# The first modulation by halves of the features, and the v product ahead of gates, q and k

## The chip, the core and the metric

The kernel runs on one core of one Trainium2 chip. The metric is the device time of one execution in microseconds. The program holds 352 MB of DMA traffic and 28,462 instructions. TensorE (PE) does matrix products, VectorE (DVE) and ScalarE (ACT) do elementwise work, GpSimd (POOL) does a little, and SyncE (SP) issues the DMAs that bring weights from memory.

## The reference

The reference is two transformer-like blocks on a sequence of 256 tokens with 1024 features, batch 1. Only the start of the first layer matters here:

```
c_act = silu(c)
mod = c_act @ ada_w[i] + ada_b[i]
sh1, sc1, g1, sh2, sc2, g2 = split(mod, 6)
h = rmsnorm(x, norm_g[i, 0]) * (1.0 + sc1) + sh1
# mlstm_mixer (layer 0):
p = h @ w_in
q, k, v, o, ig, fg = split(p)          # 512, 512, 1024, 1024, 8, 8 columns
... gates from ig, fg: cumulative decay, a running maximum, a masked decay matrix
scores = (q k^T) * decay;  num = scores @ v;  hh = num / denominator, normed
out = (sigmoid(o) * hh) @ w_out
x = x + g1 * rmsnorm(out, norm_g[i, 1])
h = rmsnorm(x, norm_g[i, 2]) * (1.0 + sc2) + sh2      # then the feed-forward part
```

`sh1` and `sc1` are one vector of 1024 numbers each, and every product of the mixer needs them. They come from `c_act` times 1024 x 1024 weights each, 4 MB for each of the two.

## The kernel before

Activations are kept transposed in SBUF: features on the 128 partitions, eight feature chunks (`KD`) of 128, and 256 tokens along the free dimension. A product in float32 accuracy is done as three fp32r products: the activation and the weight are each split into a rounded part `hi` (a ScalarE cast) and a rest `lo` (a VectorE subtraction, the method `split`), and hi*hi, hi*lo and lo*hi are summed in PSUM. `weights` loads one 1 MB tile of weights (`st`, 128 x 2048 float32) from the pool `wst`, a ring of three buffers, and makes the two pairs hi/lo of 128 x 1024. A buffer of the ring is free again when its last reader on VectorE is done.

Order in `first_block`, layer 0:

1. `ada_start` is called four times, b = 0 to 3: shift features 0 to 511, shift 512 to 1023, scale 0 to 511, scale 512 to 1023. Each call brings 2 MB of `ada_w` as four DMAs of 512 KB in two buffers `st`. Of its eight feature chunks four go through float32 matmuls against a broadcast of `c_act` (`crep`), four are summed on VectorE into `s`, and a last float32 matmul with a matrix of ones adds `s`. `diagonal` picks the column out of the PSUM tile (a product with the identity and a reduction on VectorE), and the bias is added.
2. `Finish.whole` does the RMS norm of X (`chain`: squares on ScalarE, a power on GpSimd, the scaling on VectorE and ScalarE), turns the normed rows (`turn`: float32 transposes on PE, then `hf` = scale * xn + shift) and then runs `Head`: the gate columns (40 of them) and the first two of the eight q/k blocks as float32 matmuls straight from `hf` and unsplit weights. The splits of `hf` come after.
3. `mlstm`: gates on ScalarE and VectorE, with three activation table loads; the running maximum `M` goes to memory (`md`) and comes back broadcast to all partitions (`mx`, 1.5 MB); six remaining q/k blocks by `dense_b` (24 matmuls of 256 columns each); the v product by `dense_a` (96 matmuls of 512 columns); then the o product (`a_w_o`, another 96) interleaved with the eight attention heads; then `a_w_out`.

Beside these, `self.side` holds generators for later modulations (g1, sh2, sc2). `pump` runs a step of the first of them when it is called: a step loads 1 MB of `ada_w` and multiplies it into `s` with two VectorE instructions (or a ScalarE one and a VectorE one). `mlstm` calls `pump` twice among the q/k blocks, four times in the v product and three times in the o product; the `a_w_out` product calls it with three steps at a time, and before its last weights `drain` runs whatever is left. The instructions are put in an order per engine when the program is built; each engine then runs its own in that order, and SP issues the DMAs in that order and waits where a buffer is not free.

Of the kernel before, what the change touches and what calls it, by code (L numbers as in the profile page):

```python
# [10 lines left out]
F32 = mybir.dt.float32  # L11
# [5 lines left out]
AF = mybir.ActivationFunctionType  # L17
ALU = mybir.AluOpType
# [4 lines left out]
D = 1024  # L23
KD = 8
# [251 lines left out]
class Net:  # L276
# [62 lines left out]
    def setup(self):  # L339
        nc, c, a = self.nc, self.const, self.a  # L340
        self.cols = c.tile([128, NCOL], F32, name="cols")
        nc.sync.dma_start(self.cols, a["cols"])
        self.X = self.keep.tile([128, 2, D], F32, name="X")
        k = c.tile([128, 6, 128], F32, name="kc")
        nc.sync.dma_start(k, a["k128"])
        self.junk = self.const.tile([128, D], BF16, name="junk")
        self.ident, self.ones, self.mbig, self.anti, self.bdiag, self.iota = (k[:, i] for i in range(6))
        self.cand_iota = c.tile([128, NCAND], F32, name="ciota")
        nc.sync.dma_start(self.cand_iota, a["ciota"])
# [23 lines left out]

    def weights(self, ap):

        n = ap.shape[1]
        st = self.load(ap)
# [115 lines left out]

    def ada_start(self, i, b, o):

# [5 lines left out]
        for h in range(2):  # L501
            st = self.wst.tile([128, 2048], F32, tag="st", name="st").rearrange("p (k n) -> p k n", k=4)
            for q in range(2):
                nc.sync.dma_start(st[:, 2 * q:2 * q + 2], w[2 * h + q])
            for k in range(4):
                kk = 4 * h + k
# [117 lines left out]

    def mlstm(self, x, pump, finish):
        nc, a = self.nc, self.a
        with ExitStack() as es:
# [37 lines left out]
            for n2 in range(4):  # L665
                for j, ps in enumerate(self.pair(x, a["a_w_qk"], n2, 1)):
                    n = 2 * n2 + j
# [5 lines left out]
                if n2 == 2:  # L673
# [10 lines left out]
            for t in range(2):  # L684
                for h in range(2):
                    nc.scalar.copy(v[:, t, 4 * h:4 * h + 4, :128], acc[t][h].rearrange("p (h d) -> p h d", h=4))
            hh = mp.tile([128, 2, 8, 129], F32, name="hh")
# [175 lines left out]


    def first_block(self):
        with self.tc.tile_pool(name="adap", bufs=2) as self.ada_p, self.tc.tile_pool(name="wsx", bufs=2) as self.wsx:
            m0, first, rest = self.ada_mods(0)
            with self.tc.tile_pool(name="crep", bufs=1) as p:
                self.crep = p.tile([128, KD, 128], F32, name="crep")
                self.nc.vector.tensor_copy(self.crep, self.cact.unsqueeze(2).to_broadcast([128, KD, 128]))  # L870
                for b in range(4):
                    self.ada_start(0, b, m0["sh1" if b < 2 else "sc1"][:, 4 * (b % 2):4 * (b % 2) + 4])
                    if b == 0:
                        self.nc.sync.dma_start(self.X, self.a["x"].rearrange("o (t p) d -> p (o t) d", p=128))
                o = m0["sc1"]
                self.nc.vector.scalar_tensor_tensor(o, o, 1.0, self.col("ng0_0"), op0=ALU.add, op1=ALU.mult)
            with self.tc.tile_pool(name="st0", bufs=2) as p, self.tc.tile_pool(name="work", bufs=1) as work:
# [3 lines left out]
            x = self.mlstm(fin.x, 2.0, lambda p, hst: Finish(self, p, m0["g1"], m0["sc2"], m0["sh2"], head=self.pairs(self.a["ffn_w1"][0], 4), head_pool=hst))  # L881
            m1, first, rest1 = self.ada_mods(1)
# [697 lines left out]
```

## Time and profile before

| | us |
|---|---|
| three runs, median (lowest to highest) | 1742.36 (1741.71 to 1742.83) |
| the profiled execution's own time | 1743.49 |
| its span, first to last instruction | 1741.2 |
| PE busy in the span | 1708.2 (98%) |
| DVE busy | 1378.5 (79%) |
| ACT busy | 917.5 (53%) |

The page cuts the span into 40 slices of 43.5 us. PE is busy 9 tenths or more in all but the first (7) and the last (8).

### The profile page before, as it was taken

How to read it: one execution, taken by the hardware profiler on the slowest of the kernel's cores; microseconds unless marked ns; L12 is line 12 of the kernel's file. 1: busy time of each engine (PE TensorE's matmuls, PEld its weight loads, DVE VectorE, ACT ScalarE, POOL GpSimd, SP SyncE). 2: the span in 40 equal slices, each digit the busy share in tenths (PEclk: the TensorE clock that was granted, in tenths of full speed). 3: DMA queues.
4: the chain of work that ended last, by engine and by line, in shares of the span. 5: the costliest groups of instructions: out<-in, count | busy, mean ns of one | idle time of the engine just before them, and what ended most of it. 6: DMA issues, size and time to landing. Idle time of an engine off the chain costs nothing.

```text
span 1741.2 us, 28462 instructions
## 1 busy us (share of the span) xinstructions
PE 1708.2 (98%) x11306; PEld 1508.9 (87%) x11306; DVE 1378.5 (79%) x2399; ACT 917.5 (53%) x1519; POOL 29.8 (2%) x43
## 2 busy tenths in 40 slices
PE   7999999999999999999999999999999999999998
PEld 3877888888888888999899999999888997878886
DVE  5687988679758555999867999799788948888754
ACT  3565665664456565566544445444443444445543
POOL 0000000000000000000000000000000000000000
PEclk9999999999999999999999999999999999999999
DMA  9886888558628653544355555545554455554751
GB/s 332 302 296 247 334 312 324 215 194 301 231 82 330 211 193 106 177 146 170 117 186 168 185 189 175 173 167 171 180 182 163 154 187 176 187 175 167 254 193 45
DMA packets 59599, 352.42 MB, mean 202 GB/s; under 512 B 6165, under 2 KB 12613, under 8 KB 19273
## 3 DMA queue, kind: packets, MB, share of 16 engines
q1 hardware_dynamic: 59466, 350.61, 56.7%
q8 instruction: 88, 1.44, 0.3%
q14 instruction: 45, 0.37, 0.1%
HBM read 349.51 MB, written 1.07 MB: 201 GB/s over the span
## 4 chain that ended last, share of the span: by engine, by line
PE 86%; DVE 7%; DMA 2%; ACT 2%; issue 2%; POOL 1%; SPq 0%; DVEq 0%; ACTq 0%; POOLq 0%
PE acc L113 38%; PE mm L397 10%; PE mm L399 10%; PE mm L398 10%; PE mm L426 6%; PE head L135 3%; PE mm L428 3%; DVE lo L366 2%; DVE yc L936 1%; DMA st<-in_ada_w_dram 1%; PE sd L1233 1%; PE sd L1244 1%; PE sd L512 1%; DVE ada L538 1%; DMA st<-in_a_w_v_dram 1%
## 5 line engine op out<-in xcount | busy, mean ns | idle before, releaser
L365 ACT CAST hi<-st 128x1024 fp32r<-128x1024 f32 (+1 forms) x507 | 523.8, 1049 | 434.1 <-PE mm L398 202.4
L366 DVE TENSOR_TENSOR lo<-st,hi 128x1024 fp32r<-128x1024 f32 (+1 forms) x507 | 612.6, 1222 | 146.8 <-ACT hi L365 145.2
L397 PE MATMUL mm<-h,hi 128*128 128x256 f32 x1544 | 443.1, 287 | 0.7 <-ACT qz L670 0.7
L399 PE MATMUL mm<-h,lo 128*128 128x256 f32 x1544 | 437.0, 283 | 0.9 <-DVE lo L366 0.9
L398 PE MATMUL mm<-h,hi 128*128 128x256 f32 x1544 | 436.9, 283 | 0.0
L397 PEld LDWEIGHTS mm<-h,hi 128*128 128x128 f32 x1544 | 295.4, 191 | 1.8 <-ACT qz L670 0.9
L399 PEld LDWEIGHTS mm<-h,lo 128*128 128x128 f32 x1544 | 295.3, 191 | 1.1 <-DVE lo L366 1.1
L398 PEld LDWEIGHTS mm<-h,hi 128*128 128x128 f32 x1544 | 295.5, 191 | 0.2
L113 PE MATMUL acc<-hi,h 128*128 128x512 f32 x768 | 229.7, 395 | 2.7 <-ACT h L365 1.8
L113 PE MATMUL acc<-lo,h 128*128 128x512 f32 x544 | 170.8, 391 | 0.1
L113 PEld LDWEIGHTS acc<-hi,h 128*128 128x128 f32 x768 | 141.9, 188 | 32.4 <-ACT h L365 3.2
L426 PE MATMUL mm<-h,hi 128*128 128x512 f32 x456 | 162.5, 400 | 0.0
L113 PE MATMUL acc<-hi,vh 128*128 128x512 f32 x448 | 142.5, 399 | 0.1
L113 PE MATMUL acc<-lo,vh 128*128 128x512 f32 x448 | 138.8, 391 | 0.0
L113 PE MATMUL acc<-hi,vl 128*128 128x512 f32 x448 | 137.9, 389 | 0.0
L113 PEld LDWEIGHTS acc<-lo,h 128*128 128x128 f32 x544 | 101.8, 188 | 21.8 <-DVE lo L366 0.5
L428 PE MATMUL mm<-h,lo 128*128 128x256 f32 x399 | 112.0, 281 | 0.5 <-DVE lo L366 0.5
L113 PEld LDWEIGHTS acc<-hi,vl 128*128 128x128 f32 x448 | 84.1, 188 | 18.4
L113 PEld LDWEIGHTS acc<-lo,vh 128*128 128x128 f32 x448 | 84.1, 188 | 18.1
L113 PE MATMUL acc<-hi,l 128*128 128x512 f32 x320 | 99.0, 390 | 0.0
L426 PEld LDWEIGHTS mm<-h,hi 128*128 128x128 f32 x456 | 84.1, 188 | 17.0 <-issue 0.7
L538 DVE SCALAR_TENSOR_TENSOR ada<-st,cact,ada 128x1024 f32<-128x1024 f32 x74 | 94.5, 1277 | 3.4 <-ACT ada L536 1.4
(397 smaller groups left out, 2187.7 us busy)
## 6 DMA issues: line engine op xcount, KB each, us to landing
st<-in_peer_u_dram SPq DMA_DIRECT2D x64, 1024.0 KB, 4.9
st<-in_peer_v_dram SPq DMA_DIRECT2D x64, 1024.0 KB, 4.9
st<-in_ffn_w_dram SPq DMA_DIRECT2D x62, 1024.0 KB, 6.2
st<-in_ada_w_dram SPq DMA_DIRECT2D x40, 1024.0 KB, 5.0
st<-in_ada_w_dram SPq DMA_DIRECT2D x16, 512.0 KB, 6.3
st<-in_b_w_u_dram SPq DMA_DIRECT2D x8, 1024.0 KB, 6.4
st<-in_b_w_v_dram SPq DMA_DIRECT2D x8, 1024.0 KB, 4.8
st<-in_b_w_out_dram SPq DMA_DIRECT2D x8, 1024.0 KB, 5.0
```

Of the source, the lines that this page charges most:

```text
L113: ins = mm(self.t[t][j], a[:, ts], b[:, j * 512:(j + 1) * 512], start=first and a is xh and b is wh, stop=last and a is xl)
L135: net.nc.tensor.matmul(ps[:, t * 128:(t + 1) * 128], w[:, k], x(k), start=k == 0, stop=k == KD - 1)
L365: i = self.nc.scalar.copy(hi, src)
L366: return i.ins, self.nc.vector.tensor_tensor(lo, src, hi.bitcast(F32), op=ALU.subtract).ins
L397: mm(out, ahi, bhi, start=start, stop=False)
L398: mm(out, ahi, blo, start=False, stop=False)
L399: return mm(out, alo, bhi, start=False, stop=stop)
L426: i = mm(ps, wh[:, k], x2[:, k], start=first, stop=last)
L428: i = mm(ps[:, :T], wl[:, k], xh[:, k], start=False, stop=False)
L512: nc.tensor.matmul(ps, self.crep[:, kk], st[:, k], start=kk == 0, stop=False)
L538: nc.vector.scalar_tensor_tensor(s, w, c, s, op0=ALU.mult, op1=ALU.add)
L936: nc.vector.scalar_tensor_tensor(y[:, n], up[:, n, w:w + T], self.col("conv_w", n * 31 + w), y[:, n], op0=ALU.mult, op1=ALU.add)
```

## The change

`ada_start` is called in the order 0, 2, 1, 3, so that shift and scale of features 0 to 511 come first. A new function `lead` replaces `Finish.whole`. It loads X ahead of most of the weights, norms both token tiles into buffers of their own, transposes and modulates features 0 to 511 (`turn(0)`, `scaled(0)`), and runs the v product over the first half of the features (`product(0)`, `product(1)`: 48 matmuls) around the third `ada_start`; after the fourth it modulates features 512 to 1023 and runs the other half of v. The weights of v go through a pool of two buffers of their own (`st0`). `mlstm` gets the finished accumulators of v, computes the gates as a split fp32r product and all eight q/k blocks by `dense_b`. `Head` is not used there any more. The constants are cut in parts that are loaded at three times. `mlstm` calls `pump` once after each q/k pair and three times in the o product.

```diff
-        nc.sync.dma_start(self.cols, a["cols"])
...
+        c8 = c.tile([128, KD], F32, name="c8")
+        nc.sync.dma_start(c8, a["cols"][:, :KD])
...
-        nc.scalar.activation(self.cact, self.col("c"), AF.Silu)
+        nc.scalar.activation(self.cact, c8, AF.Silu)
+    def fetch(self):
+        nc.sync.dma_start(self.k2, a["k128"][:, :2])
+        nc.sync.dma_start(self.X, a["x"].rearrange("o (t p) d -> p (o t) d", p=128))
+        nc.sync.dma_start(self.cols, a["cols"])
...
-    def mlstm(self, x, pump, finish):
+    def mlstm(self, x, acc, pump, finish):
...
+            for t in range(2):
+                for h in range(2):
+                    nc.scalar.copy(v[:, t, 4 * h:4 * h + 4, :128], acc[t][h].rearrange("p (h d) -> p h d", h=4))
...
-            ps = self.head.ps[0]
+            w = self.weights(a["a_w_g"])[0]
+            ps = self.dense_b(x, [t.rearrange("p (k m) -> p k m", k=KD) for t in w], m=40)
...
-                for j, ps in enumerate(self.pair(x, a["a_w_qk"], n2, 1)):
+                for j, ps in enumerate(self.pair(x, a["a_w_qk"], n2)):
...
-                if n2 >= 2:
-                    self.pump(pump)
-
-            acc = self.dense_a(x, a["a_w_v"], pump=pump)
...
+                self.pump(pump)
...
+            self.ada_start(0, 0, sh[:, :4], self.fetch)
+            self.ada_start(0, 2, sc[:, :4])
+            for t in range(2):
+                chain(t)
+            pss = turn(0)
+            scaled(0, pss)
+            pss = turn(1)
+            product(0, st0)
+            self.ada_start(0, 1, sh[:, 4:])
+            product(1, st0)
+            self.ada_start(0, 3, sc[:, 4:])
+            scaled(1, pss)
+            product(2, st0)
+            product(3, st0)
+            self.fetch_more()
...
-                for b in range(4):
-                    self.ada_start(0, b, m0["sh1" if b < 2 else "sc1"][:, 4 * (b % 2):4 * (b % 2) + 4])
...
-                fin = Finish(self, work, None, m0["sc1"], m0["sh1"], head=[(self.a["a_w_g"], 1, 40)] + self.pairs(self.a["a_w_qk"], 2), head_pool=p)
-                fin.whole()
+                v = self.lead(m0)
```

On PE, before, the last modulation matmuls (`sd<-st,crep`, and with the ones `sd<-ada,kc`) and the transposes stand ahead of the float32 head, and the first q/k block follows:

```order
L203 MATMUL mm<-kc,xn 128x128 x4
L512 MATMUL sd<-st,crep 128x512 x2
L513 MATMUL sd<-ada,kc 128x512
L203 MATMUL sd<-kc,xn 128x128 x4
L135 MATMUL head<-hf,st 40x128 x8
L135 MATMUL head<-hf,st 128x128 x16
```

On PE, now, where the v product (`acc<-hi,h_121`) begins: it stands between matmuls of the third modulation part.

```order
L528 MATMUL sd<-ada,kc 128x512
L527 MATMUL sd<-st,crep 128x512
L909 MATMUL mm<-kc,xn_122 128x128 x4
L909 MATMUL mm<-kc,xn_123 128x128 x4
L527 MATMUL sd<-st,crep 128x512
L113 MATMUL acc<-hi,h_121 128x512 x4
```

Further on, now, at the end of the first half of v and the start of the second (the matmuls with the ones, L528, stand directly ahead of the second half):

```order
L113 MATMUL acc<-hi,h_121 128x512 x2
L527 MATMUL sd<-st,crep 128x512 x4
L528 MATMUL sd<-ada,kc 128x512
L113 MATMUL acc<-hi,h_121 128x512 x2
L113 MATMUL acc<-lo,h_121 128x512 x2
```

The head is gone from this place, and the four matmuls of the fourth modulation part come after all 48 of the first half of v.

On VectorE, before, in the last product of the mixer (`a_w_out`): `ada_1000` is the sum for sc2, `lo_1194` and `lo_1218` belong to the second and third MB of `a_w_out`.

```order
L749 TENSOR_TENSOR og_1095<-og_1095,hh_748 128x512 x2
L538 SCALAR_TENSOR_TENSOR ada_1000<-st_1187,cact_96,ada_1000 128x1024
L366 TENSOR_TENSOR h2_1104<-sd_1112,h2_1104 128x4x128
L366 TENSOR_TENSOR lo_1194<-st_1191,hi_1193 128x1024
L366 TENSOR_TENSOR h2_1104<-sd_1126,h2_1104 128x4x128
L366 TENSOR_TENSOR lo_1198<-st_1191,hi_1197 128x1024
L550 TENSOR_REDUCE sc2_0_107<-sd_1201 128x4
L366 TENSOR_TENSOR lo_1218<-st_1215,hi_1217 128x1024
```

On VectorE, now, at the same place (`ada_1216` is the sum for sc2, `lo_1228` the second MB of `a_w_out`, `lo_1246` the third):

```order
L379 TENSOR_TENSOR lo_1228<-st_1221,hi_1227 128x1024
L379 TENSOR_TENSOR h2_1124<-sd_1146,h2_1124 128x4x128
L553 SCALAR_TENSOR_TENSOR ada_1216<-st_1231,cact_96,ada_1216 128x1024
L565 TENSOR_REDUCE sh2_0_106<-sd_1203 128x4
L567 TENSOR_TENSOR sh2_0_106<-sh2_0_106,cols_86 128x8
L553 SCALAR_TENSOR_TENSOR ada_1216<-st_1235,cact_96,ada_1216 128x1024 x2
L553 SCALAR_TENSOR_TENSOR ada_1216<-st_1239,cact_96,ada_1216 128x1024 x2
L379 TENSOR_TENSOR lo_1246<-st_1243,hi_1245 128x1024
L565 TENSOR_REDUCE sc2_0_107<-sd_1253 128x4
```

Two more loads of the side work, and the end of sh2, have moved into this product, and six multiply-adds stand between the second and the third MB of its weights.

## Rows read from the trace of the kernel before

**Rows 1.** The page: span, busy time, chain of work that ended last

```profile
span 1741.2 us, 28462 instructions
PE 1708.2 (98%) x11306; PEld 1508.9 (87%) x11306; DVE 1378.5 (79%) x2399; ACT 917.5 (53%) x1519; POOL 29.8 (2%) x43
PE 86%; DVE 7%; DMA 2%; ACT 2%; issue 2%; POOL 1%; SPq 0%; DVEq 0%; ACTq 0%; POOLq 0%
```

**Rows 2.** Busy time by stage: stretch, length, engines, granted clock, DMA share, GB/s

```profile
core 0: us, PE busy (x) PEld busy (x) DVE busy (x) ACT busy (x) POOL busy (x), PEclk, DMA share, GB/s
36.30:49.40 13.10, 13.03 (x97) 11.68 (x97) 10.28 (x17) 8.34 (x16) 0.00 (x0) 0.87 0.95 342
49.40:93.50 44.10, 42.66 (x253) 36.76 (x252) 31.42 (x32) 25.16 (x39) 2.10 (x3) 1.00 0.84 306
93.50:128.40 34.90, 33.41 (x183) 28.36 (x181) 31.27 (x65) 23.98 (x66) 4.08 (x3) 1.00 0.81 292
128.40:156.80 28.40, 24.90 (x117) 19.49 (x116) 22.69 (x37) 11.87 (x20) 1.67 (x3) 1.00 0.78 309
```

**Rows 3.** The same view, short stretches around the start of the head

```profile
10.00:15.00 5.00, 4.93 (x8) 1.72 (x6) 1.43 (x3) 0.59 (x2) 0.00 (x0) 1.00 1.03 403
34.00:35.00 1.00, 0.21 (x3) 0.20 (x3) 0.91 (x2) 0.00 (x0) 0.00 (x0) 1.00 1.28 250
38.00:39.00 1.00, 1.00 (x6) 0.89 (x5) 0.54 (x2) 1.00 (x4) 0.00 (x0) 0.50 0.99 410
41.00:42.00 1.00, 1.00 (x11) 1.00 (x11) 1.00 (x3) 1.00 (x2) 0.00 (x0) 1.00 1.05 262
```

**Rows 4.** Timeline of the start: start, length, engine, line, operation, [idle before]

```profile
7.34 6.74 PE L512 MATMUL sd<-st,crep 128*128 128x512 f32 x8 [7.34 <-DMA st<-in_ada_w_dram]
...
8.59 0.75 DVE L510 SCALAR_TENSOR_TENSOR ada<-st,cact,ada 128x512 f32<-128x512 f32 x1 [0.87 <-DMA st<-in_ada_w_dram]
...
14.41 0.63 ACT L164 ACTIVATE junk<-X 128x512 bf16<-128x512 f32 x1 [11.04 <-DMA X<-in_x_dram]
...
17.54 0.72 ACT L192 ACTIVATE xn<-X,rs_r 128x512 f32<-128x512 f32 x1 [1.18 <-POOL rs_r L170]
...
32.99 1.02 PE L513 MATMUL sd<-ada,kc 128*128 128x512 f32 x2
...
34.05 0.69 DVE L521 TENSOR_TENSOR adad<-sd,kc 128x512 f32<-128x512 f32 x1 [1.22 <-PE sd L513]
...
35.90 2.90 ACT L216 ACTIVATE hf<-mm,sh,sc 128x128 f32<-128x128 f32 x8 [5.19 <-DVE sc L876]
...
38.65 2.21 ACT L365 CAST h<-hf 128x512 fp32r<-128x512 f32 x4
...
40.72 3.92 ACT L365 CAST hi<-st 128x1024 fp32r<-128x1024 f32 x4
```

**Rows 5.** Timeline of PE: the head here, q/k blocks, a later head, 512-column matmuls

```profile
36.37 13.26 PE L135 MATMUL head<-hf,st 128*40 128x128 f32 x96 [0.91 <-DVE hf L212]
...
49.70 0.28 PE L399 MATMUL mm<-h,lo 128*128 128x256 f32 x1
...
49.82 0.28 PE L397 MATMUL mm<-h,hi 128*128 128x256 f32 x1
...
147.30 1.75 PE L113 MATMUL acc<-hi,h 128*128 128x512 f32 x7
...
159.71 7.31 PE L135 MATMUL head<-hf,st 128*128 128x128 f32 x64
```

**Rows 6.** Timeline: the gates' maximum goes to memory, and its broadcast is used

```profile
57.13 0.30 SPq L653 DMA_DIRECT2D md<-M  x1
...
68.16 1.22 DVE L659 TENSOR_TENSOR mx<-mx,kc 128x1024 f32<-128x1024 f32 x1 [0.23 <-DMA mx<-md]
```

**Rows 7.** Timeline of the last product of the mixer: PE's largest wait, a side step

```profile
135.59 1.06 PE L484 MATMUL sd<-kc,og 128*128 128x128 f32 x8 [1.37 <-DVE og L749]
...
135.97 1.28 DVE L538 SCALAR_TENSOR_TENSOR ada<-st,cact,ada 128x1024 f32<-128x1024 f32 x1
```

More of the change, by code (lines that the diff above doesn't have):

```diff
@@ L372, in load, with weights @@
         return st
-    def weights(self, ap):
+    def weights(self, ap, stage=None):
         n = ap.shape[1]
-        st = self.load(ap)
+        st = self.load(ap, stage)
         out = []
@@ L504, in ada_start @@
                 nc.sync.dma_start(st[:, 2 * q:2 * q + 2], w[2 * h + q])
+            if h == 0:
+                then()
             for k in range(4):
@@ L862, in sgu, with lead, chain, turn @@
         return fin.x
+    def lead(self, m0):
+        nc, a = self.nc, self.a
+        sh, sc, ng = m0["sh1"], m0["sc1"], self.col("ng0_0")
+        with self.tc.tile_pool(name="st0", bufs=2) as st0, self.tc.tile_pool(name="work", bufs=1) as p:
+            x = self.h_tiles()
+            xn = [p.tile([128, D], F32, name=f"xn{t}") for t in range(2)]
+            acc = Acc(self, KD, tail=2)
+            def chain(t):
+                X = self.X[:, t]
+                ss = self.small.tile([128, 2], F32, tag="ss", name="ss")
+                for h in range(2):
+                    hs = slice(h * 512, (h + 1) * 512)
+                    nc.scalar.activation(self.junk[:, hs], X[:, hs], AF.Square, scale=1.0 / 32.0, accum_out=ss[:, h:h + 1])
+                v = self.small.tile([128, 1], F32, tag="rs_v", name="rs_v")
+                nc.vector.tensor_scalar(v, ss[:, 0:1], ss[:, 1:2], EPS, op0=ALU.add, op1=ALU.add)
+                r = self.small.tile([128, 1], F32, tag="rs_r", name="rs_r")
+                nc.gpsimd.tensor_tensor(r, v, self.mhalf, op=ALU.pow)
+                nc.vector.tensor_scalar(xn[t][:, :512], X[:, :512], r, None, op0=ALU.mult)
+                nc.scalar.activation(xn[t][:, 512:], X[:, 512:], AF.Copy, scale=r)
+            def turn(h):
+                pss = []
+                for t in range(2):
+                    ps = self.mm_tile().rearrange("p (k c) -> p k c", k=4)
+                    for k in range(4):
+                        kk = 4 * h + k
+                        nc.tensor.transpose(ps[:, k], xn[t][:, kk * 128:(kk + 1) * 128], self.ident)
+                    pss.append(ps)
+                return pss
+            def scaled(h, pss):
+                hs = slice(4 * h, 4 * h + 4)
+                nc.vector.scalar_tensor_tensor(sc[:, hs], sc[:, hs], 1.0, ng[:, hs], op0=ALU.add, op1=ALU.mult)
+                for t, ps in enumerate(pss):
+                    hf = p.tile([128, 4, 128], F32, tag="hf", name="hf", bufs=2)
+                    for k in range(4):
+                        gk, sk = sc[:, 4 * h + k:4 * h + k + 1], sh[:, 4 * h + k:4 * h + k + 1]
+                        if t == 0:
+                            nc.vector.tensor_scalar(hf[:, k], ps[:, k], gk, sk, op0=ALU.mult, op1=ALU.add)
+                        else:
+                            nc.scalar.activation(hf[:, k], ps[:, k], AF.Identity, scale=gk, bias=sk)
+                    o = (slice(None), hs, slice(t * 128, (t + 1) * 128))
+                    self.hi, self.lo = self.split(x[0][o], x[1][o], hf)
+            def product(k2, pool=None):
+                for j, w in enumerate(self.weights(a["a_w_v"][k2], pool)):
+                    k = 2 * k2 + j
+                    acc.add((x[0][:, k], x[1][:, k]), w)
+            self.ada_start(0, 0, sh[:, :4], self.fetch)
+            self.ada_start(0, 2, sc[:, :4])
+            for t in range(2):
+                chain(t)
[10 more added lines that the diff above has]
+            self.fetch_more()
+        return x, acc.t
@@ L870, in first_block @@
                 self.nc.vector.tensor_copy(self.crep, self.cact.unsqueeze(2).to_broadcast([128, KD, 128]))
[L871 to L879 removed]
+                v = self.lead(m0)
             self.side = rest[:3]
[L881 removed]
+            x = self.mlstm(*v, 2.0, lambda p, hst: Finish(self, p, m0["g1"], m0["sc2"], m0["sh2"], head=self.pairs(self.a["ffn_w1"][0], 4), head_pool=hst))
             m1, first, rest1 = self.ada_mods(1)
```

19 lines of the change are left out of this document (11 added, 8 removed).

## Prediction

> **What bounds the kernel now.** I read the page first: PE is busy for 98% of the span and holds 86% of the chain that ended last [rows 1]. So the time is PE's work plus the little that PE waits, and a change counts by what it does to those two until the last place where order differs, the end of the mixer at about 157 us. After that both kernels run the same program, PE-bound, and a lead or a lag at 157 us is carried to the end.
>
> Next the view of busy time by stage [rows 2]. The reader is to see four stages behind the modulation: the float32 head (36.3 to 49.4, at a mean granted clock of 0.87), q/k blocks and v (44.1 us, PE idle 1.4), the o product with the heads (34.9, idle 1.5) and the last product `a_w_out` (28.4, idle 3.5). Before 36.4 us PE only does float32 modulation matmuls and transposes, and DMA moves 403 GB/s [rows 3]. The largest wait of PE is there, not behind it.
>
> Then the timeline of the start [rows 4]: the first 512 KB of `ada_w` let PE go at 7.3 us, X is there at 14.4, and the last matmul with the ones begins at 33.0; 2.9 us later ScalarE writes `hf`. The head runs from 36.4 [rows 5].
>
> **The change, part by part.** All times count from the span's start, and I build the new sequence by adding durations of these rows.
>
> *Weights at the start.* Ahead of the first `ada_w` now lie 4 KB of constants instead of 0.59 MB (331 + 768 + 54 float32 on 128 partitions, from the diff). At 0.403 MB per us [rows 3] that is 1.5 us, and two issues fewer at 0.3 each [rows 6] give 0.6: the first 512 KB land at about 5 us. X ends 1.7 MB later, at 9.3. All that the first half of the features needs is 5.55 MB, so it lands at 5 + 5.03/0.403 = 17.5 us.
>
> *First half of the modulation.* DVE does not reach that DMA time, because the norm of X stands in its order among the modulation sums. X to the first `xn` takes 3.9 us (14.4 to 18.3 [rows 4]); the second tile, by the same kinds of instruction, about 2.4 more: 15.6 us. Then one sum (0.75), the ones (1.02), product and reduction (2 x 0.69), three sums (0.75 each) lead to 21.2, where the second matmul with the ones begins. From there to `hf` it takes 2.9 us as before [rows 4]: 24.1. ScalarE writes four `hf` (half of 2.90), makes two casts of h (0.55 each) and one of weights (0.98): PE can begin v at 27.6 us. I allow 26.5 to 29.
>
> *First half of v on PE.* 48 matmuls of 512 columns at 0.227 us each (seven end 1.75 after their start, the last with a tail of 0.39 [rows 5]) are 10.9 us. Between them stand eight float32 matmuls of the other two modulation parts, at about 0.87 each (bounded by the 1.02 with tail [rows 4]): 7.0. PE is through at 45.5 us. No transfer is late for it: by bytes the fourth part is there at about 35 us.
>
> *The new wait.* The second `hf` needs the ones that begin at 44.6, so it starts at 47.5; `hf`, casts of h and of weights follow (1.45 + 1.1 + 0.98): 51.0. PE has nothing else in its order there (gates and q/k stand behind v and need all of h), so it idles 5.5 us. Queued behind this wait are all of v's second half, gates and q/k.
>
> *TensorE's clock.* Before, PE was busy 0.21 of the stretch 34 to 35, and the granted clock then fell to 0.50 (1.2 GHz) at 38 to 39 and was 1.00 (2.4 GHz) again at 41 to 42 [rows 3]; the head's mean of 0.87 over 13.1 us [rows 2] costs 1.7 us at most. The 5.5 us gap is longer, so I charge 1.4 us for one fall after it, and 0.7 (half a chance of another) for the thin stretch before 27.6. The Trainium skill ("TensorE: Matmul & The Clock Gate", section "HAM oscillation — how this bites in real kernels") says that PE waits between bursts bring the throttled clock back, so that each burst starts cold; that speaks against a change that cuts the lead into two bursts. By that rule both falls come and the sum would be 0.7 us higher; the row shows one fall after one thin stretch.
>
> *Gates, q and k.* The head goes: 96 instructions in 13.1 us, of which 10.9 is work at full clock (64 in 7.31 [rows 5]). In its place come three blocks of 24 fp32r matmuls at 0.12 (from 49.70 to 49.82 [rows 5]), 8.6 us: 2.3 us less work. Second half of v 10.9 with the clock's 2.1: v ends at 64.0; nine blocks (25.9) and four tiny transposes: 90.1 us. Before, this point was 93.5. But the two float32 matmuls of g1 (1.8) now come behind it, since side steps moved: the work done is ahead by 1.6 us only.
>
> *Side work.* `pump` is called seven times ahead of `a_w_out` instead of nine. So two steps, 2 MB of `ada_w` and four multiply-adds (one on ScalarE), and the end of sh2 (eight transposes, 0.9 us at the head's rate, and two reductions) go from the earlier stages into `a_w_out`. The o stage: 34.9 + 1.8 - 0.9, less 0.8 of its 1.5 idle (some of it stood behind sh2's reductions) = 35.0: end at 125.1 against 128.4. In the last stage PE's largest wait is for `og` (1.37 [rows 7]), which DVE has ready 7.6 us into the stage; one multiply-add fewer stands ahead of it: 6.3. Behind it DVE has about 4.3 of splits, six multiply-adds of 1.28 [rows 7] and two reductions (1.3): it hands sc2's sum to PE 19.5 us into the stage. PE is there after 17.0 (6.2 for the first transposes and their wait, 35 matmuls 7.9, 20 transposes and their waits 2.9), waits 2.5, and has 0.9 + 48 x 0.227 = 11.8 left: 31.3 instead of 28.4. Bounds of this 2.9 us: +0.9, if only the transposes count, and +10.4, if both loads come in series (2.6 of transfer and 2.6 of DVE each). I take 2.9, near the rows' order. It takes back nearly all.
>
> *Constants, v copies, mask.* The copies of v move from before the o product to behind v: ScalarE was idle for much of that stage (25.2 of 44.1 busy [rows 2]), so 0; if not, up to 4 x 0.5 from the cast row's half. Later constants: not needed before `mx`, 0.
>
> **Sum.** 125.1 + 31.3 = 156.4 against 156.8 where the stage ended: -0.4, I say -0.5 us. Against the profiled execution's 1743.5 that is 1743.0; the runs' median is 1.1 lower, so I predict 1741.9. Unknown are the start of v (1.2 either way), the clock (-2.1 to +2), the last stage (-2 to +7.5).
>
> **Rivals.**
>
> *The gain stays (faster).* No clock is lost after the gap, and the side steps hide in the last stage but for their 0.9. Then 2.1 and 2.0 come on top: -4.6, 1737.8. For it: DMA moves only 309 GB/s of 403 in the last stage [rows 2, 3] and DVE idles 5.7 us there; against: DVE's multiply-adds now stand ahead of the third MB's split.
>
> *The ring of three buffers (slower).* `a_w_out`'s third and fourth MB get their buffers only when DVE has used the side loads ahead of them. If each such load costs transfer plus DVE in turn, the last stage takes 7.5 us more than I gave it: up to +7, at half of that +3.3; I price the case at +5, 1747.4. It decides from the point where sc2's sum is ready 23.5 us into the stage or later. For it: the order; against: two loads are in flight at a time.
>
> *The gates' chain comes late (slower).* Before, `M` left at 57.1 and its mask was added at 68.2 [rows 6], 25 us ahead of its use. Now it leaves about 9.6 us after v's end (7.7 as from the head's end before, and two copies of v), and by the same 12.2 us to the masked `mx`, six exponentials (2.5) and a cast the first o weights are ready 25.3 us after v's end; PE wants them at 27.5. With 2.2 us of cover it costs nothing; from 6.2 late it makes the kernel slower, and 7 late gives +4.3, 1746.7.
>
> *It does not do what it says:* if the first half of v waited for the second half's weights, v would run from 51 on: 10.9 us later on PE, 1752. Nothing in the order asks for that, so it gets almost no weight.
>
> **How the numbers follow.** What counts as no change is 0.2%, 3.5 us on 1742.4. Forecast, 1738.9 to 1745.9: 0.49. The gain stays: 0.28. The ring: 0.14. The gates' chain: 0.08; the last rival: 0.01. So faster 0.28, same 0.49, slower 0.23. The range reaches into both sides: from 1736.5 (below the first rival's 1737.8 by the start of v) to 1747.4, the ring's price.
>
> **What would show it.** In the changed kernel's timeline: v's first matmul at 26.5 to 29; a PE gap of 4 to 7 us near 45 to 51 that ends with the ScalarE cast, and a granted clock of 0.50 behind it; the o product from 88 to 92; the end of `a_w_out`'s matmuls within 3 us of 156.8; PE waiting for DVE at sc2's transposes. If the gap is absent, or the last stage takes less than 30 us, I am wrong towards faster; if it takes over 35, or PE waits for the first o weights, towards slower.

## The result: 12 us slower, and the profile after

The changed kernel takes 1754.83 us (median of 4 runs, 1754.31 to 1756.86) against 1742.58 for the kernel before: ratio 1.0069, 95% interval 1.0056 to 1.0081. The forecast was no change, 1741.9; the time lies above the range.

The page of the profile after (span; PE's busy time; the chain that ended last), to be held against [rows 1]:

```profile
span 1752.6 us, 28431 instructions
PE 1713.2 (98%) x11282; PEld 1513.3 (86%) x11282; DVE 1381.6 (79%) x2403; ACT 920.1 (52%) x1522; POOL 32.6 (2%) x43
PE 87%; DVE 7%; ACT 2%; issue 1%; DMA 1%; POOL 1%; SPq 0%; DVEq 0%; ACTq 0%; POOLq 0%
```

The span grew by 11.4 us. PE's idle time is the span less its busy time: 33.0 before, 39.4 now, +6.4. PE's busy time grew by 5.0, although PE has 24 instructions fewer. An instruction that takes longer points to the clock.

Busy time by stage in the kernel after (columns as in [rows 2]):

```profile
36.30:49.40 13.10, 12.29 (x42) 7.48 (x40) 4.62 (x9) 0.00 (x0) 0.00 (x0) 1.00 0.64 214
49.40:94.20 44.80, 39.94 (x269) 36.51 (x269) 33.63 (x39) 29.60 (x48) 2.10 (x3) 0.92 0.78 286
94.20:129.80 35.60, 34.75 (x182) 28.67 (x180) 30.48 (x62) 24.60 (x66) 6.01 (x3) 1.00 0.74 269
129.80:164.20 34.40, 28.30 (x129) 22.40 (x128) 28.41 (x44) 11.24 (x19) 1.94 (x2) 0.95 0.86 336
```

Against [rows 2] the o stage begins 0.7 us later, takes 0.7 longer, and the last product 6.0 longer (34.4 for 28.4). The granted clock is 0.92 and 0.95 where it was 1.00. Short stretches of the same view show where it was low:

```profile
28.00:31.00 3.00, 3.00 (x8) 1.71 (x7) 3.00 (x5) 3.00 (x4) 0.00 (x0) 0.52 1.00 388
53.00:58.00 5.00, 3.74 (x8) 2.54 (x9) 4.83 (x6) 5.00 (x7) 0.00 (x0) 0.50 0.31 129
151.00:154.00 3.00, 3.00 (x12) 2.61 (x11) 2.21 (x2) 2.52 (x3) 0.00 (x0) 0.50 1.02 426
168.00:171.00 3.00, 3.00 (x16) 3.00 (x16) 2.15 (x5) 2.47 (x8) 0.00 (x0) 0.51 0.43 178
```

There are four falls to 1.2 GHz where [rows 3] show one. Busy time by (1 - clock) is what a fall took from PE: 1.4 + 1.9 + 1.5 + 1.5 = 6.3 us in these four stretches, and 7.2 with their edges (windows of 2 us: 1.7, 2.3, 1.5 and 1.7); the fall before took 1.6 by the same windows. Each stands behind a wait of PE. Timeline of PE in the kernel after (idle before the row and its releaser in brackets; 67.61 is the first matmul of the gates, 94.20 the first of the scores):

```profile
13.05 2.08 PE L527 MATMUL sd<-st,crep 128*128 128x512 f32 x2 [3.26 <-DMA st<-in_ada_w_dram]
...
27.16 1.12 PE L909 MATMUL mm<-kc,xn 128*128 128x128 f32 x8 [2.31 <-ACT hf L923]
...
29.28 1.14 PE L113 MATMUL acc<-hi,h 128*128 128x512 f32 x1
...
47.57 1.02 PE L528 MATMUL sd<-ada,kc 128*128 128x512 f32 x2
54.22 1.22 PE L113 MATMUL acc<-hi,h 128*128 128x512 f32 x2 [5.63 <-ACT hi L378]
...
67.61 0.28 PE L410 MATMUL mm<-h,hi 128*40 128x256 f32 x1
...
94.20 0.60 PE L711 MATMUL sd<-qz,kT 128*128 128x256 f32 x2
...
150.64 1.63 PE L564 MATMUL sd<-kc,ada 128*128 128x128 f32 x8 [2.73 <-DVE ada L553]
...
166.44 0.33 PE L203 MATMUL mm<-kc,xn 128*128 128x128 f32 x1 [2.21 <-ACT xn L192]
```

Behind the last product PE is 7.4 us late (164.2 for 156.8); X's transposes wait 2.21 (1.12 before), the head behind them starts at half clock, and `ffn` begins 9.7 us late. The last 1.7 us of the lag come from a fall between 856 and 862 us, behind code that is the same in both kernels:

```profile
856.00:862.00 6.00, 5.83 (x36) 5.62 (x36) 3.77 (x8) 2.51 (x4) 0.70 (x1) 0.72 0.01 3
```

With it the falls took 8.9 us of PE's busy time in the whole execution, against 1.6 before. That is 7.3 more, and less 2.3 us of work (the forecast's figure for the head's loss) it gives the 5.0 by which PE's busy time grew. The 6.4 of idle time make up the rest of the 11.4. The late fall need not belong to the change: profiles of `no_head_filled` and `before_consts_late`, which keep the old order, have one like it at 840 to 846 us.

### The profile page after: what moved, and what is told of

Read it like the earlier page. It is cut to its first block, busy times and chain, and to the rows that moved or that the text cites. A ratio compares the mean times of both kernels' runs of the same rounds, so it can differ in the third digit from the quotient of the medians.

```text
span 1752.6 us, 28431 instructions
## 1 busy us (share of the span) xinstructions
PE 1713.2 (98%) x11282; PEld 1513.3 (86%) x11282; DVE 1381.6 (79%) x2403; ACT 920.1 (52%) x1522; POOL 32.6 (2%) x43
## 3 DMA queue, kind: packets, MB, share of 16 engines
HBM read 349.52 MB, written 1.07 MB: 200 GB/s over the span
## 4 chain that ended last, share of the span: by engine, by line
PE 87%; DVE 7%; ACT 2%; issue 1%; DMA 1%; POOL 1%; SPq 0%; DVEq 0%; ACTq 0%; POOLq 0%
PE acc L113 39%; PE mm L410 10%; PE mm L411 10%; PE mm L412 10%; PE mm L439 6%; PE head L135 3%; PE mm L441 3%; DVE lo L379 2%; DVE yc L1012 1%; PE sd L1309 1%; PE sd L1320 1%; PE sd L527 1%; DMA st<-in_ada_w_dram 1%; DVE ada L553 1%; PE sd L855 0%
## 5 line engine op out<-in xcount | busy, mean ns | idle before, releaser
L410 PE MATMUL mm<-h,hi 128*128 128x256 f32 (+1 forms) x1568 | 449.8, 287 | 0.0
L412 PE MATMUL mm<-h,lo 128*128 128x256 f32 (+1 forms) x1568 | 443.7, 283 | 0.9 <-DVE lo L379 0.9
L411 PE MATMUL mm<-h,hi 128*128 128x256 f32 (+1 forms) x1568 | 443.6, 283 | 0.0
L410 PEld LDWEIGHTS mm<-h,hi 128*128 128x128 f32 (+1 forms) x1568 | 299.4, 191 | 1.2 <-issue 0.6
L412 PEld LDWEIGHTS mm<-h,lo 128*128 128x128 f32 (+1 forms) x1568 | 299.3, 191 | 1.1 <-DVE lo L379 1.1
L411 PEld LDWEIGHTS mm<-h,hi 128*128 128x128 f32 (+1 forms) x1568 | 299.5, 191 | 0.3
L441 PE MATMUL mm<-h,lo 128*128 128x256 f32 x399 | 112.1, 281 | 0.5 <-DVE lo L379 0.5
L439 PEld LDWEIGHTS mm<-h,hi 128*128 128x128 f32 x456 | 84.1, 188 | 17.0 <-issue 0.7
```

The costliest lines, as they stand in the source:

```text
L410: mm(out, ahi, bhi, start=start, stop=False)
L411: mm(out, ahi, blo, start=False, stop=False)
L412: return mm(out, alo, bhi, start=False, stop=stop)
L439: i = mm(ps, wh[:, k], x2[:, k], start=first, stop=last)
L441: i = mm(ps[:, :T], wl[:, k], xh[:, k], start=False, stop=False)
```

## The experiments

Each kernel ran beside the kernel before; the ratio is to that. "Lost" is the sum of (1 - granted clock) times 2 us over windows of 2 us from 20 to 190 us of the profiled execution; it counts idle time too. Ahead of 20 us five profiles have another fall that is not in the column (`before_seven_steps` 1.0; `parts_first` and `one_burst_filled` 1.7; `before_consts_late` and `two_steps_no_dve` 3.4). "Scores" is where the first scores start in the same execution; in the old order that is inside the v product, in the kernel before 5.0 us ahead of the o product. "Last" is the length of the last product. These three columns are of one execution, which is not always near the median: that of `nine_steps` took 1751.02 us, that of `one_burst` 1751.11.

| kernel | median us | ratio, interval | lost | scores | last |
|---|---|---|---|---|---|
| before | 1742.6 to 1743.9 | 1 | 1.7 | 88.6 | 28.3 |
| after | 1754.83 | 1.0069 [1.0056, 1.0081] | 8.5 | 94.2 | 34.4 |
| nine_steps | 1754.11 | 1.0065 [1.0050, 1.0079] | 5.1 | 97.3 | 29.6 |
| before_seven_steps | 1748.73 | 1.0031 [1.0019, 1.0043] | 5.8 | 89.2 | 33.0 |
| parts_first | 1754.07 | 1.0062 [1.0047, 1.0078] | 8.6 | 87.6 | 37.1 |
| parts_first_nine | 1749.32 | 1.0036 [1.0024, 1.0048] | 3.4 | 96.7 | 29.7 |
| gap_filled | 1752.35 | 1.0059 [1.0046, 1.0072] | 3.4 | 91.4 | 34.6 |
| one_burst | 1754.41 | 1.0071 [1.0058, 1.0084] | 6.8 | 91.1 | 34.5 |
| two_steps_no_dve | 1750.29 | 1.0045 [1.0031, 1.0059] | 5.1 | 95.2 | 30.7 |
| two_steps_small_loads | 1754.38 | 1.0069 [1.0056, 1.0082] | 8.5 | 94.4 | 37.1 |
| waits_filled | 1750.40 | 1.0037 [1.0023, 1.0051] | 3.4 | 90.1 | 36.3 |
| nine_small_loads | 1749.60 | 1.0032 [1.0018, 1.0045] | 5.1 | 95.9 | 29.6 |
| before_consts_late | 1744.26 | 0.9999 [0.9987, 1.0011] | 0 | 89.5 | 28.3 |
| before_no_head | 1749.43 | 1.0030 [1.0019, 1.0041] | 5.1 | 91.8 | 29.1 |
| no_head_seven_steps | 1748.65 | 1.0030 [1.0018, 1.0041] | 6.8 | 92.1 | 32.7 |
| before_ten_steps | 1744.99 | 1.0010 [1.0001, 1.0019] | 3.4 | 84.4 | 28.7 |
| parts_nine_spare | 1748.51 | 1.0037 [1.0025, 1.0049] | 3.4 | 95.9 | 28.8 |
| no_head_filled | 1744.12 | 1.0005 [0.9997, 1.0014] | 0 | 88.8 | 28.3 |
| one_burst_filled | 1752.16 | 1.0052 [1.0039, 1.0065] | 5.1 | 90.0 | 35.9 |
| before_spare | 1745.66 | 1.0014 [1.0005, 1.0023] | 0 | 88.4 | 28.3 |

**The displaced side steps.** `nine_steps` adds to the changed kernel's q/k loop:

```diff
+                if n2 >= 2:
+                    self.pump(pump)
                 self.pump(pump)
```

> The changed kernel with nine instead of seven side steps ahead of the last product (one step more behind each of the third and fourth pair of q and k). Theory A, the displaced side steps: the two steps that the change moved into the last product cost it its 6 us and, by the waits there, the clock falls behind it. Then the last product goes from 34.5 back to 28.5 to 31 us, the wait of PE for sc2's sum and the falls at 151 and 168 us go, and the whole is 6 to 10 us shorter than the changed kernel (1745 to 1749). Theory B, the lead in two bursts costs it (the gap of 5.6 us at 48.6 and the clock after it, which only hid behind an earlier start): the whole stays within 2 us of the changed kernel (1753 to 1757), since nothing ahead of 68 us is touched.

The last product came back to 29.6 us and its falls went, as theory A said, but the scores start 3.1 later and the median is unchanged, as theory B said. In the profiled execution the mixer still ends 1.0 earlier (163.2 for 164.2) and `ffn` begins 3.1 earlier; the other four executions were 2 to 5 us longer than that one. So the trace shows that most of the gain is paid back among q and k, and not where the rest of it goes. `before_seven_steps` takes `if n2 >= 2: self.pump(pump)` out of the kernel before.

> The kernel before, with two side steps fewer ahead of the last product (the two behind the third and fourth pair of q and k are left to it), so that its 18 steps divide as in the changed kernel; nothing else is changed. Theory A: slower than the kernel before by 5 to 10 us (1748 to 1753), with PE waiting in the last product for sc2's sum. Theory B: within 2 us of the kernel before (1741 to 1745).

+5.7 us, in theory A's range, but not by the wait that it named: PE has no wait for sc2's sum there. Its longest in the last product is for `og`:

```profile
130.01 0.63 PE L484 MATMUL sd<-kc,og 128*128 128x128 f32 x4 [2.18 <-DVE og L747]
```

Its last product is 4.7 longer and its stretch from the scores to there 3.9 shorter (125.2 less 89.2, for 128.5 less 88.6), so the mixer ends only 1.4 later (158.2 for 156.8). "Lost" is 5.8 for 1.7. That points to the clock behind the waits for much of the price; no run fills these waits.

To see what a displaced step uses, the last two of sc2 lost first VectorE's products, then most of their loads (with products of the same size over the 64 columns that are left; these lines are not shown):

```diff
-            for k in range(2):
+            for k in range(0 if (i, b) == (0, 4) and h >= 2 else 2):
```

```diff
-            st = self.load(self.a["ada_w"][i, b, h], self.ast)
+            few = (i, b) == (0, 4) and h >= 2
+            st = self.load(self.a["ada_w"][i, b, h][:, :64] if few else self.a["ada_w"][i, b, h], self.ast)
```

> The changed kernel without VectorE's four products of the last two steps of sc2 (1.3 us each); their loads of 1 MB each remain. Left out: half of the sum behind sc2. It prices the displaced steps by their engine. If VectorE's time in the o stage and the last product is what they cost (theory A): the last product goes from 34.5 to 28 to 30 us and the whole is 5 to 9 us shorter (1746 to 1750). If it is their loads (theory C): the last product stays at 32 us or more and the whole within 3 us of the changed kernel.

> The counterpart: the changed kernel with the loads of the last two steps of sc2 cut from 1 MB each to 32 KB each, and VectorE's four products of the same size over what is loaded, repeated. Left out: the weights of these two steps. Theory C (loads): the last product at 28 to 30 us and the whole 5 to 9 us shorter than the changed kernel. Theory A (VectorE's time): 33 us or more, the whole within 3 us of it.

Without VectorE's products the last product takes 30.7 us and the time is 4.5 shorter, just short of what theory A asked for (30 and 1750 at most); the interval overlaps the changed kernel's slightly. Small loads leave the time as it was (1754.38) and the last product is even longer (37.1). That run does not price the loads alone: a load of `ffn_w` moves ahead of `a_w_out`'s third load, whose cast begins at 153.00 us instead of 150.71 although it is issued as before (145.45 for 145.24). The changed kernel's own rows say what VectorE does: four multiply-adds in a row on DVE (second row) set the end of PE's wait at 150.64, and the one ahead of them (first row) sets, on SyncE's queue, the start of `a_w_out`'s third load, which needs the buffer that it frees:

```profile
143.94 1.27 DVE L553 SCALAR_TENSOR_TENSOR ada<-st,cact,ada 128x1024 f32<-128x1024 f32 x1
...
145.24 5.25 DVE L553 SCALAR_TENSOR_TENSOR ada<-st,cact,ada 128x1024 f32<-128x1024 f32 x4
```

```profile
129.17 3.61 SPq L384 DMA_DIRECT2D st<-in_ada_w_dram  x2
...
140.83 0.33 SPq L384 DMA_DIRECT2D st<-in_ada_w_dram  x1
145.24 0.33 SPq L384 DMA_DIRECT2D st<-in_a_w_out_dram  x1
```

Among q and k the loads are the first suspect. `nine_small_loads` is `nine_steps` with the same cut for `(i, b) == (0, 2)`, the two steps that now stand there.

> The changed kernel with nine side steps ahead of the last product, the loads of two of them (the last two of g1, which now fall behind the third pair of q and k) cut from 1 MB to 32 KB each, VectorE's four products over what is loaded, repeated, as long as before. Left out: the weights of these two steps. It asks why nine steps don't help: in their run the scores started 3.1 us later (97.3), while the last product was 4.8 us shorter. Theory C (the q and k stretch, 72 to 92 us, is bound by its loads, with the DMA share at 1.0): scores start at 93 to 95 us and the whole is 4 to 7 us shorter than with nine full steps (1747 to 1750). Theory A (VectorE's time): scores stay at 96 us or later, the whole within 2 us of nine full steps (1752 to 1756).

4.5 us shorter than with full loads, as theory C said; the scores start at 95.9 for 97.3, short of the 93 to 95 that it asked for. PE busy in the q/k stretch with full loads (first fence) and with small ones:

```profile
84.00:88.00 4.00, 4.00 (x30) 3.44 (x30) 3.74 (x5) 0.96 (x3) 0.00 (x0) 1.00 1.06 418
88.00:92.00 4.00, 1.98 (x8) 0.85 (x7) 1.33 (x2) 4.00 (x9) 0.00 (x0) 1.00 0.95 399
```

```profile
84.00:88.00 4.00, 3.94 (x35) 3.71 (x33) 4.00 (x4) 1.80 (x4) 0.00 (x0) 1.00 0.97 408
88.00:92.00 4.00, 3.66 (x20) 2.70 (x21) 4.00 (x7) 4.00 (x9) 0.00 (x0) 1.00 0.67 227
```

With full loads the DMA share is about 1.0 and PE is busy for 1.98 of 4 us; with small ones for 3.66. Another difference stands beside the loads: ScalarE's order. In `nine_steps` the cast that PE waits for comes behind five exponentials, of which the first waits for VectorE; in `nine_small_loads` the casts come ahead of them:

```profile
87.81 0.51 ACT L710 ACTIVATE e<-mx,ac 128x256 f32<-128x256 f32 x1 [0.53 <-DVE ac L701]
...
89.61 1.97 ACT L378 CAST hi<-st 128x1024 fp32r<-128x1024 f32 x2
```

```profile
86.15 1.05 ACT L378 CAST hi<-st 128x1024 fp32r<-128x1024 f32 x1 [1.00 <-DMA st<-in_a_w_qk_dram]
```

So that the loads are the cause there is likely, not shown.

**The lead.** `parts_first` moves one call, and `parts_first_nine` has both edits:

```diff
-            product(1, st0)
             self.ada_start(0, 3, sc[:, 4:])
+            product(1, st0)
             scaled(1, pss)
```

> The changed kernel with the fourth part of the first modulation computed ahead of v's second chunk of weights instead of behind it, so that 24 matmuls of v stand between the last ones-product and the modulated second half. Theory B: PE's gap of 5.6 us ahead of v's second half falls under 1.5 us, the clock doesn't fall at 52 us, the o product's scores start at 87 to 90 instead of 94.2 us, and the whole is 5 to 8 us shorter than the changed kernel (1747 to 1750). Theory A: the start comes earlier by the same 4 to 7 us, but the last product still waits for its side steps, 34 us or more long, and gives back half or more: the whole is 0 to 3 us shorter.

> Both edits at once: the fourth part ahead of v's second chunk, and nine side steps ahead of the last product. Theory A and theory B together (both costs are real and stand apart): 11 to 17 us shorter than the changed kernel, 1738 to 1744, so at or below the kernel before. Theory A alone: as with nine steps, 1745 to 1749. Theory B alone: as with the parts first, 1747 to 1750.

With the part first, the gap of 5.6 us became 0.87, with 1.00 more inside the first half, and the scores start 6.6 us earlier, as both theories said. The time is theory A's: o stage and last product are 4.7 longer (falls at 128 to 136 took part), 1.9 is left at the mixer's end, and the median is 0.8 shorter with overlapping intervals. Only with nine steps does it pay: 5.5 shorter, where each edit alone gave 0.7 or 0.8. That was below what the sum of A and B asked for (11 to 17).

`one_burst` undoes the halves: parts 1 and 3 go ahead of `scaled(0, pss)`, and `product(0)` behind `scaled(1, pss)`.

> The changed kernel with the lead in one burst: all four parts of the first modulation are computed ahead of the first matmul of v, both halves are modulated at once and v follows in one piece; gates, q and k stand behind v as in the changed kernel, with seven side steps ahead of the last product. It undoes the halves and keeps the new order of the products. Theory B (the halves cost it): scores start by 92 and the whole is 4 us or more shorter than the changed kernel. Theory C: the order of the products and the seven steps are what costs, so the whole stays within 2 us of the changed kernel or is up to 4 us longer, with the last product still 33 us or more.

No difference to the changed kernel in the median, as theory C said, though the scores start 3.1 earlier, as theory B said. Its timeline shows that the halves had not removed the gap, only put it between two bursts; in one burst it is as long:

```profile
33.93 1.02 PE L528 MATMUL sd<-ada,kc 128*128 128x512 f32 x2
40.59 1.22 PE L113 MATMUL acc<-hi,h 128*128 128x512 f32 x2 [5.64 <-ACT hi L378]
```

`before_consts_late` is the kernel before with the split constants and `fetch` alone.

> The kernel before with one part of the change alone: only 4 KB of constants ahead of the first weights, ident, ones and X behind their first half, the rest of the constants later. Nothing else moves. All theories: the first modulation matmul at 5.5 instead of 7.3 us, and if VectorE and the loads keep that lead, the whole is 1 to 2.5 us shorter than the kernel before (1740.5 to 1742); if the last ones-product is bound by loads that only changed places, no difference (1742.5 to 1743.5).

No difference: this part of the change is neither gain nor loss.

**The clock.** `gap_filled` puts spare matmuls behind part 4 (its edit follows); `waits_filled` does so at all four thin places:

```diff
             self.ada_start(0, 3, sc[:, 4:])
+            idle = self.sd_tile()
+            for i in range(6):
+                nc.tensor.matmul(idle, self.ident, xn[0][:, :512], start=i == 0, stop=i == 5)
             scaled(1, pss)
```

> The changed kernel with six spare float32 matmuls (128x512, into an accumulator that nobody reads) put into PE's gap ahead of v's second half; they take about 5 us there. Theory B (the clock falls in the gap and costs what stands behind it): PE isn't idle from 48.6 to 54.2 us, the clock doesn't fall at 52 us, v ends 3 to 3.5 us earlier (64 to 65) and the o product's scores start at 90 to 92 instead of 94.2. By theory B the whole is then 3 to 4 us shorter than the changed kernel (1750 to 1752); by theory C (what the first 165 us have to load comes through three staging buffers, and PE's start only waits for it later) the end moves by less than 1.5 us, the last product being longer by what the start gains.

> The changed kernel with spare float32 matmuls (128x512, into accumulators that nobody reads) at four thin places of PE: two behind the second ones-product of the lead (ahead of 27 us), six in the gap ahead of v's second half, three in the last product near sc2's transposes, two ahead of the first transposes of X behind the last product. By the records the changed kernel lost 8.5 us of PE time to the clock up to 190 us (sum over 2 us windows of one minus the granted clock), the kernel before 1.7. Theory B (the clock): the loss falls under 3 us and the whole is 4 to 7 us shorter than the changed kernel (1748 to 1751). Theory A (VectorE's side steps and the buffers set the pace of the last product): the loss falls as well, but PE waits instead, and the whole is at most 3 us shorter (1752 to 1755).

The fall at 53 to 58 went and the scores start 2.8 earlier; of it 2.5 reached the end, between the two theories and with overlapping intervals. All four filled give 4.4, in theory B's range, and here the intervals stand apart. In the profiled executions the span is 6.2 shorter and the falls take 3.0 us of PE's busy time instead of 8.9, so that the clock accounts for nearly all of this difference. In `waits_filled` the four stretches are at full clock, but another fall came at 130 to 136:

```profile
28.00:32.00 4.00, 3.84 (x15) 2.43 (x14) 4.00 (x5) 3.44 (x4) 0.00 (x0) 1.00 1.02 367
52.00:58.00 6.00, 5.53 (x23) 4.27 (x24) 5.83 (x8) 5.46 (x7) 0.87 (x1) 1.00 0.11 48
130.00:136.00 6.00, 5.05 (x14) 3.52 (x13) 4.44 (x9) 1.24 (x2) 0.82 (x1) 0.53 0.53 184
151.00:155.00 4.00, 4.00 (x18) 2.99 (x17) 4.00 (x5) 2.50 (x3) 0.00 (x0) 1.00 1.00 422
168.00:172.00 4.00, 4.00 (x39) 4.00 (x38) 1.77 (x5) 1.38 (x4) 1.05 (x2) 1.00 0.17 66
```

**The float32 head.** `before_no_head` takes from the kernel before what the change also took:

```diff
-... head=[(self.a["a_w_g"], 1, 40)] + self.pairs(self.a["a_w_qk"], 2), head_pool=p)
+... head=[], head_pool=p)
```

with gates from `dense_b` and `self.pair(x, a["a_w_qk"], n2)`; `no_head_filled` adds five spare matmuls in the gap that opens.

> The kernel before without the float32 head: gates and the first two pairs of q and k are computed from converted halves (three fp32r products, as in the changed kernel), in the order of before, with nine side steps. It isolates the cost of the head's loss, five more conversions on ScalarE and VectorE (1.2 us each) and PE waiting for the split of x, from the order of the products. Theory A/C (VectorE and the loads pace the kernel up to the last product): slower than the kernel before by 4 to 9 us (1747 to 1752), about the same as the changed kernel with the fourth part and nine steps (1749). Theory B (the clock in the two-burst lead is the cost): within 3 us of the kernel before (1741 to 1746), since the lead is one burst.

> The kernel before without the float32 head, and with five spare float32 matmuls (128x512, into an accumulator that nobody reads) in the gap of 4.6 us (35.7 to 40.3) that the head's loss opened ahead of the first product. In the run without them the clock fell there and 5.1 us of PE time went by 48 us. If the head was worth its price as a cover that keeps the clock up: the fall goes and the whole comes back by 3 to 5 us, to 1744.5 to 1746.5. If what the head's loss costs is the wait and the five added conversions: within 1.5 us of the run without spare matmuls (1748 to 1751).

Without the head +5.7 us; with the head gone and the gap filled by work that nobody reads, within 0.1% of the kernel before. Windows of the two, first without and then with the spare matmuls:

```profile
36.00:40.00 4.00, 0.00 (x0) 0.00 (x0) 3.21 (x8) 4.00 (x11) 0.00 (x0) 0.59 0.40 164
40.00:44.00 4.00, 3.45 (x15) 2.66 (x16) 4.00 (x7) 3.99 (x5) 2.09 (x3) 0.50 0.53 123
44.00:48.00 4.00, 4.00 (x24) 3.71 (x23) 1.81 (x2) 1.42 (x2) 0.00 (x0) 0.63 1.00 395
```

```profile
36.00:40.00 4.00, 3.35 (x9) 1.63 (x9) 3.20 (x9) 4.00 (x11) 0.00 (x0) 1.00 0.46 188
40.00:44.00 4.00, 3.90 (x25) 2.80 (x24) 4.00 (x8) 4.00 (x6) 2.10 (x3) 1.00 0.44 112
44.00:48.00 4.00, 4.00 (x36) 3.99 (x35) 2.20 (x2) 3.70 (x5) 0.00 (x0) 1.00 1.00 378
```

In the first 8 us DVE and ACT do the same and DMA moves about as much: the split of x takes its time in both. What differs is the clock of what follows. In the kernel before, the head did useful work in that place: the clock fell at its start (0.50 at 38 to 39) and was back at 1.00 before its end [rows 3]. `no_head_seven_steps` has both edits of before at once, `one_burst_filled` seven spare matmuls in the gap of `one_burst`.

> The kernel before with both edits at once: without the float32 head, and with seven side steps ahead of the last product. The lead stays in one burst and gates, q and k stay ahead of v. If the two costs add and make up the whole lag of the changed kernel: 1752.5 to 1757, the changed kernel's 1754.8. If the halves and the order of the products cost something of their own, or the two costs share one wait: 1748 to 1751.

> The changed kernel with the lead in one burst, and seven spare float32 matmuls (128x512, into an accumulator that nobody reads) in the gap of 5.6 us ahead of v (35 to 40.6). If the clock in the gap makes its difference to the kernel before without head (1748.65): the fall of 36 to 45 us goes (4.6 us of PE time in the run without spare matmuls) and the whole is 1748.5 to 1751. If the order of the products does it by side steps and loads: 1753 to 1755.

The two prices do not add: 1748.65, no more than either. And filling the gap of `one_burst` gave only 2.3 us, between both forecasts and with overlapping intervals; the fall in the lead went, but those at 132 us and at X's transposes stayed, and one at 150 came new.

**Ways past the kernel before.** `before_ten_steps` writes `n2 >= 1` for `n2 >= 2`; `before_spare` puts two spare matmuls in the short waits ahead of the head.

> The kernel before with ten side steps ahead of the last product, one more behind the second pair of q and k. If a step moved out of the last product is worth what one moved into it cost (5.7 us for two): 1740 to 1741.5. If the last product of before no longer waits for sc2 (PE's waits there are for the product og and for casts), the step buys nothing there and adds its load to the stretch ahead: 1742 to 1746, the scores up to 2 us later.

> The kernel before, its head kept, with two spare float32 matmuls (128x512, into an accumulator that nobody reads) in PE's two short waits ahead of the head (34.0 to 36.4 us). If the fall of 36 to 41 us, 1.7 us of PE time in the profiled run, goes and nothing else is late: 1741 to 1742, 1 to 2 us under the kernel before. If PE's start of the head hid behind data that came no earlier: within 0.7 us of it.

Neither helps: +2.0 and +1.7 us. A tenth step has nothing left to free, since the last product of before does not wait for sc2. The second miss is explained in part: its fall is gone, and the first q/k block starts 1.6 us earlier (47.78 for 49.38), but the scores start only 0.2 earlier (88.38 for 88.55) and `ffn` as well. From there to the scores PE waits 2.6 us for casts and copies of ScalarE, for 1.4 before. So the time that a fall's absence gives can go into the next wait; why the median is 1.7 longer stays open. `parts_nine_spare` (`parts_first_nine` with two spare matmuls ahead of 27 us) took 1748.51, 0.8 less than without them and no difference at these intervals; its forecasts were 1746 to 1748.5 if the gain is kept and 1748.5 to 1750.5 if q and k take it back. No kernel that I ran is faster than the kernel before.

## Why the prediction was wrong

The forecast's stages against the trace of the kernel after (us from the span's start; the last column is what each stage added to the miss):

| point | forecast | measured | added |
|---|---|---|---|
| first matmul of v | 27.6 | 29.3 | 1.7 |
| PE through the first half | 45.5 | 48.6 | 1.4 |
| second half of v starts | 51.0 | 54.2 | 0.1 |
| v ends | 64.0 | 67.6 | 0.4 |
| o product starts | 90.1 | 94.2 | 0.5 |
| o product ends | 125.1 | 129.8 | 0.6 |
| last product ends | 156.4 | 164.2 | 3.1 |
| span, against before | -0.4 | +11.4 | 4.0 |

- *TensorE's clock.* This is the step that failed. The sum charged 2.1 us, for one fall and half a chance of another, both in the lead. Five came and took 8.9 us of PE's busy time: 4.0 in the lead, 1.5 in the last product, 1.7 in the head behind X, 1.7 near 857 us. That is 6.8 of the 11.8 us by which the span was missed. The forecast had PE's wait for sc2 (2.5 us) and put no fall behind it. The sentence on the Trainium skill's rule ("TensorE: Matmul & The Clock Gate", section "HAM oscillation — how this bites in real kernels") was right against my half chance: both bursts of v in the lead started at about 0.50 of the clock (0.52 at 28 to 31, 0.50 at 53 to 58). The trace doesn't bear it out after every wait: behind the 3.26 us ahead of 13.05 the clock stayed at 1.00. By experiment, spare matmuls in four of these places give back 4.4 us of the median.
- *Side work in the last product* is the second miss: 34.4 us for 31.3, within the bounds of +0.9 to +10.4. The mechanism was right (PE's wait for sc2 2.73 for 2.5, its sum 20.8 us into the stage for 19.5). The rival of the buffers' ring was partly right, since `a_w_out`'s third load waits for VectorE, but the sum came well ahead of the 23.5 us from which it was to decide. Of the 3.1 the clock at 150 to 156 is 1.5. "Work ahead by 1.6 us" left out that moved steps cost something wherever they stand.
- *Weights at the start, first half, the new wait.* The structure was right: the gap was 5.63 for 5.5 and closed by the cast. It came 3.2 late: v's first matmul came at 29.28, outside the 26.5 to 29 allowed, since the second matmul with the ones began at 22.5 for 21.2, and PE ran part of the first half at half clock.
- *Gates, q and k.* As a term of the sum this held: 26.6 us from v's end to the scores for 26.1, and PE's busy time fits 2.3 us less work. The scores are 4.1 late because 3.6 of it stood ahead of the gates. What the forecast did not ask is what the head covered. On the kernel before alone its loss costs 5.7 us, not a gain of 2.3, and spare matmuls in its place give that back; in the changed kernel the sum had the wait that opens (the gap), but too little clock behind it.
- *Behind 157 us* the prediction had nothing; X's wait and the head's start at half clock added 2.3 us up to `ffn`, and the late fall 1.7.
- *The gates' chain* came in time, as forecast; so that rival fell. *The constants* cost nothing, as forecast.

Shown: on the kernel before, the head's loss costs by the clock; in the changed kernel, spare matmuls in PE's waits give back 4.4 us; VectorE's products of the displaced steps cost 4.5, with slightly overlapping intervals; the halves leave the gap as it was. Open: these prices do not add up in any run. With lead and side steps both treated the changed kernel stays at 1748.5 to 1749.3, and I found no run that recovers the last 5 to 6 us. Open too is why seven steps without a head cost 1748.65 in the old order of the products and 1754.41 in the new one (`one_burst`), though their profiled executions end the last product at 161.1 and 161.4 us: the difference lies in executions that were not profiled, whose mean clock is lower (0.990 to 0.995 for 0.995 to 0.997).

## What to carry to other kernels

Before taking work off PE ahead of a wait, ask what that work covers: if the engine idles in its place, the clock behind may cost more than the work did. Count every wait of PE that an edit creates, also stages later, as a possible fall of the clock, and price it from a fall in the trace: here one took 1.5 to 2.3 us. Side work that moves is not free at its new place: look there for the resource (loads, VectorE, staging buffers) that is already full.

## What the runs showed of the hardware

- In the kernel after, waits of PE of 2.31, 5.63, 2.73 and 2.21 us were each followed by 3 to 6 us at 0.50 of the clock. The wait's length alone does not decide. The wait of 3.26 us ahead of 13.05 was not followed by a fall. X's wait of 2.21 or 2.22 us stands in nine profiles, with a fall behind it in six and none in three (`gap_filled`, `two_steps_no_dve`, `two_steps_small_loads`). And three short waits in a row (1.40, 0.68 and 0.95 us from 126 to 132 us of `waits_filled`) came with 0.53 at 130 to 136, where the kernel after had 1.41, 0.68 and 1.07 us in the same place and stayed at 1.00. A fall behind a wait is likely, not certain.
- Executions of one kernel differ, in part with the clock: those of `one_burst` run from 1751.11 us at a mean clock of 0.995 to 1759.57 at 0.990, but those of `nine_steps` at 0.996 took 1751.02 to 1756.12.
- Matmuls whose result nobody reads hold the clock up as well as useful ones: five of them took the kernel without its head from 1749.43 to 1744.12 us.
